# Row-wise infinity norm: the last quarter of the rows in smaller pieces, and the results stored in three parts

## The chip, the core and the metric

The kernel runs on one core of a Trainium2 chip. What counts is the device time of one execution in microseconds (us). Before the change it is 644.95 us, the median of 3 runs (644.83 to 644.98).

## What is computed

The input x is a matrix of 8192 rows and 8192 columns of float32 (268.4 MB). For each row the kernel returns the largest absolute value in it, 8192 numbers in all:

```python
x = np.random.randn(8192, 8192).astype(np.float32)
return np.linalg.norm(x, ord=np.inf, axis=1)
```

Each element is read once and used in one comparison, so this is a stream through the on-chip memory: 128 partitions, each of which holds some rows.

## The kernel before

The rows are cut into A = 8 blocks of 1024 rows. In a block each partition owns 8 consecutive rows. A block is loaded in N = 4 steps; a step loads B = 2 rows per partition, that is, 128 partitions by 64 KB, 8.39 MB, into one tile `t`. There are 32 such tiles in all, one after the other in the loops on lines 45 and 47 (the branch `if split` is never taken, since `split` is False).

Two engines take part, and the DMA engines between them:

- SP (SyncE) issues the load of each tile on line 70, all on its own DMA queue, and waits in program order. The pool `sbuf` (line 39) has three buffers. So the load of tile i+3 waits until the reduce of tile i has read the buffer.
- DVE (VectorE) reduces a tile with one instruction (lines 71 to 76) of 128 partitions by 16384 elements, which gives two maxima per partition, one for each row. They go to `r_all`, which holds all results on chip.
- When all 32 tiles are reduced, SP stores `r_all` with one DMA (line 78). It is made of runs of 8 floats (32 bytes): 8 blocks times 128 partitions, 1024 runs.

Each DMA signals its completion on a semaphore. There are eight of them, named `DMAHW0` to `DMAHW7`, which the framework hands to the DMAs in turn. A DMA that gets one of them again has to wait until the DMA that had it before is complete. In the listings below, a name in brackets is a wait, and the `_49` behind it belongs to the name alone. A wait on `DVE_49` is one for reduces that are done with.

Of the kernel before, what the change touches and what calls it, by code (L numbers as in the profile page):

```python
# [1 line left out]
logging.getLogger("concourse").setLevel(logging.ERROR)  # L3

# [1 line left out]

# [4 lines left out]


@with_exitstack
def kernel(
    ctx: ExitStack,
    tc: tile.TileContext,
    x: bass.AP,
    out: bass.AP,
    A: int = 8,
    B: int = 2,  # L20
    K: int = 4,
    BUFS: int = 3,
):
    nc = tc.nc
    P = nc.NUM_PARTITIONS

    rows, cols = x.shape
    assert rows % P == 0
    n_tiles = rows // P

    assert n_tiles % (A * B) == 0
    N = n_tiles // (A * B)
    x_t = x.rearrange("(a p n b) c -> a n p (b c)", p=P, a=A, n=N, b=B)
    out_t = out.rearrange("(a p n b) -> p a n b", p=P, a=A, n=N, b=B)

    bc = cols * B
    c_k = bc // K

    sbuf = ctx.enter_context(tc.tile_pool(name="sbuf", bufs=BUFS))
    outp = ctx.enter_context(tc.tile_pool(name="outp", bufs=1))  # L40

    r_part = outp.tile([P, N, K], mybir.dt.float32)
    r_all = outp.tile([P, A, N, B], mybir.dt.float32)

    for a in range(A):
        split = False
        for n in range(N):
            t = sbuf.tile([P, bc], x.dtype)
            t_b = t.rearrange("p (b c) -> p b c", b=B, c=cols)
            src = x_t[a, n]  # L50
            if split:
                for k in range(K):
                    nc.sync.dma_start(
                        out=t[:, k * c_k : (k + 1) * c_k],
                        in_=src[:, k * c_k : (k + 1) * c_k],
                    )
                    nc.vector.reduce_max(
                        out=r_part[:, n, k : k + 1],
                        in_=t[:, k * c_k : (k + 1) * c_k],
                        axis=mybir.AxisListType.X,  # L60
                        apply_absolute_value=True,
                    )
                nc.vector.reduce_max(
                    out=r_all[:, a, n, :],
                    in_=t_b[:],
                    axis=mybir.AxisListType.X,
                    apply_absolute_value=True,
                )
            else:
                nc.sync.dma_start(out=t[:], in_=src)  # L70
                nc.vector.reduce_max(  # L71
                    out=r_all[:, a, n, :],
                    in_=t_b[:],
                    axis=mybir.AxisListType.X,
                    apply_absolute_value=True,
                )

    nc.sync.dma_start(out=out_t[:], in_=r_all[:])


# [1 line left out]
_INS = ['x']  # L82
_OUTS = [((8192,), 'float32')]


# [23 lines left out]
```

## Time and profile before

| | |
|---|---|
| median of 3 runs | 644.95 us |
| span of the profiled execution, first to last instruction | 643.6 us |
| difference: what lies around the span | 1.35 us |
| DVE busy | 551.0 us, 32 reduces of 17.22 us |
| moved by the DMA engines | 268.47 MB, 417 GB/s over the span |
| last load landed, last reduce started | 623.38 us |
| last reduce ended, store issued | 640.6 us |

The profile is that of one execution. Its own time is its span, 643.6 us; the runs that were timed are 1.35 us longer, since they hold what lies ahead of the first instruction and behind the last. The DMA share is the mean busy share of 16 DMA engines. In short windows it goes above 1 and below it, as packets of 64 KB are counted where they are recorded; over 100 us it can be read as it stands. The chain of waits is followed back from the last instruction, at each step to what released it; where a load is in that chain, its time is from issue to landing, with what was queued ahead of it.

### The profile page before, as it was taken

The page shows a single profiled execution, that of the slowest core. Times are in us where ns is not written, and L with a number is a line of the kernel's source. Part 1 is how long each engine was busy: PE and PEld are TensorE (multiplying, and loading weights), DVE is VectorE, ACT ScalarE, POOL GpSimd, SP SyncE. Part 2 cuts the span into 40 slices and gives each one's busy share as a digit, 9 for nine tenths or more (in the row PEclk, how much of TensorE's full clock was granted, in tenths as well). Part 3 has the DMA queues.
Part 4 walks back from the last instruction along what each step waited for, and adds up shares of the span by engine and source line. Part 5 has one row for each costly group of instructions (what it writes and reads, how often), then busy time and mean ns, then how long its engine had stood idle before and what let it go on. Part 6 is the DMA issues. An engine that isn't in the chain of part 4 may idle for free.

```text
span 643.6 us, 139 instructions
## 1 busy us (share of the span) xinstructions
DVE 551.0 (86%) x32; POOL 0.2 (0%) x4
## 2 busy tenths in 40 slices
DVE  0588898888998888998888988888988888988888
POOL 0000000000000000000000000000000000000000
DMA  9999999999999999999999999999999999999960
GB/s 391 456 399 448 444 403 456 391 456 444 403 456 444 403 456 440 407 456 436 411 456 432 415 456 424 424 456 407 440 456 399 448 452 399 452 444 403 456 261 2
DMA packets 5648, 268.47 MB, mean 417 GB/s; under 512 B 1552, under 2 KB 1552, under 8 KB 1552
## 3 DMA queue, kind: packets, MB, share of 16 engines
q1 hardware_dynamic: 5648, 268.47, 96.6%
HBM read 268.44 MB, written 0.03 MB: 417 GB/s over the span
## 4 chain that ended last, share of the span: by engine, by line
DMA 70%; DVE 29%; issue 0%; SPq 0%
DMA t<-in_x_dram 70%; DVE r_all L71 29%; SPq L70 0%
## 5 line engine op out<-in xcount | busy, mean ns | idle before, releaser
L71 DVE TENSOR_REDUCE r_all<-t 128x2 f32<-128x16384 f32 x32 | 551.0, 17220 | 89.6 <-DMA t<-in_x_dram 89.6
L93 POOL MEMSET const-bfloat16-1.0<- 128x1 bf16 x1 | 0.1, 102 | 0.0
L93 POOL MEMSET const-uint8-127<- 128x1 uint8 x1 | 0.1, 102 | 0.0
L93 POOL MEMSET const-float32-0.0<- 128x1 f32 x1 | 0.1, 99 | 0.2 <-issue 0.2
L93 POOL MEMSET const-float32-1.0<- 128x1 f32 x1 | 0.1, 99 | 0.0
## 6 DMA issues: line engine op xcount, KB each, us to landing
t<-in_x_dram SPq DMA_DIRECT2D x32, 40.8
out_dram<-r_all SPq DMA_DIRECT2D x1, 32.0 KB, 2.2
```

The costliest lines, as they stand in the source:

```text
L71: nc.vector.reduce_max(out=r_all[:, a, n, :], in_=t_b[:], axis=mybir.AxisListType.X, apply_absolute_value=True,)
L93: nc = _bacc.Bacc("TRN2", target_bir_lowering=False, num_devices=1)
```

## The change

The first 48 of every 64 rows (24 of the 32 tiles) are loaded and reduced as before, into `r_bulk`. Their results are stored by one DMA that is issued from the queue of ACT (ScalarE) as soon as the 24th reduce is done.

The remaining 2048 rows are the tail: 16 rows per partition. A table `TAIL` says in which pieces each of the 16 rows is loaded: eight rows whole (8192 elements, 32 KB per partition), five rows in two pieces of 4096, two rows in four pieces of 2048, and the last row in pieces of 2048, 2048, 2048, 1024, 512 and 512 elements (2 KB per partition). Two rows still share a buffer, so the tail has 8 buffers' worth of data in 32 DMAs. Each piece has its own reduce. The partial maxima go to `part`, which is set to zero at the start; one more small reduce turns it into the results of 15 rows, `r_tail`, stored from ACT's queue. The partial maxima of the last row are written behind the row's own data in the buffer (which got 16 more elements for this), so that the last reduce reads the last piece and the five maxima as one run of 517 elements. Its result, `r_fin`, is stored by SP: 128 partitions by 4 bytes.

In the tail each partition owns 16 consecutive rows, so that neighbouring partitions read 512 KB apart in HBM; in the rest they read 256 KB apart, as before.

```diff
+TAIL = (
+    [[8192]] * 8
+    + [[4096, 4096]] * 5
+    + [[2048] * 4] * 2
+    + [[2048, 2048, 2048, 1024, 512, 512]]
+)
...
-    x_t = x.rearrange("(a p n b) c -> a n p (b c)", p=P, a=A, n=N, b=B)
-    out_t = out.rearrange("(a p n b) -> p a n b", p=P, a=A, n=N, b=B)
...
+    x_b = x[:split].rearrange("(a p n b) c -> a n p (b c)", p=P, a=A, n=G, b=B)
+    out_b = out[:split].rearrange("(a p n b) -> p a (n b)", p=P, a=A, n=G, b=B)
+    x_t = x[split:].rearrange("(p t b) c -> t p (b c)", p=P, b=B)
+    out_t = out[split:].rearrange("(p t) -> p t", p=P)
...
+    part = outp.tile([P, n_tail - 1, k_max], F32)
+    nc.vector.memset(part[:], 0.0)
+
+    def absmax(o, i):
+        nc.vector.reduce_max(out=o, in_=i, axis=X, apply_absolute_value=True)
 
     for a in range(A):
...
+        for n in range(G):
+            t = sbuf.tile([P, B * cols + 16], F32, tag="t")
+            nc.sync.dma_start(out=t[:, : B * cols], in_=x_b[a, n])
+            absmax(
+                r_bulk[:, a, n * B : (n + 1) * B],
+                t[:, : B * cols].rearrange("p (b c) -> p b c", b=B),
+            )
+    nc.scalar.dma_start(out=out_b, in_=r_bulk[:])
+
+    for i in range(0, n_tail, B):
+        t = sbuf.tile([P, B * cols + 16], F32, tag="t")
+        for j in range(B):
+            r = i + j
+            at = j * cols
+            last = r == n_tail - 1
+            for k, w in enumerate(TAIL[r]):
+                nc.sync.dma_start(
+                    out=t[:, at : at + w], in_=x_t[i // B][:, at : at + w]
+                )
+                if last and k == k_last - 1:
+
+                    absmax(r_tail[:, : n_tail - 1], part[:])
+                    nc.scalar.dma_start(
+                        out=out_t[:, : n_tail - 1], in_=r_tail[:, : n_tail - 1]
                     )
+                    absmax(r_fin[:], t[:, at : B * cols + k_last - 1])
+                elif last:
+                    absmax(
+                        t[:, B * cols + k : B * cols + k + 1], t[:, at : at + w]
                     )
+                else:
+                    absmax(part[:, r, k : k + 1], t[:, at : at + w])
+                at += w
+    nc.sync.dma_start(out=out_t[:, n_tail - 1 :], in_=r_fin[:])
```

Two places in the order of the instructions matter below. The first is on SP, the engine that issues all loads, where the tail has begun. Before, the last loads there were these, one per tile, each behind the reduce that frees its buffer, with the one store behind them:

```order
L70 DMA t<-in_x_dram 128x16384 [waits DMAHW1_49,DVE_49]
L70 DMA t<-in_x_dram 128x16384 [waits DMAHW2_49,DVE_49]
L70 DMA t<-in_x_dram 128x16384 [waits DMAHW3_49,DVE_49]
L70 DMA t<-in_x_dram 128x16384 [waits DMAHW4_49,DVE_49]
L78 DMA out_dram<-r_all 128x8x8 [waits DVE_49]
```

Now, on SP, the third, fourth and fifth tile of the tail (27th to 29th of all 32) are issued so:

```order
L82 DMA t<-in_x_dram 128x8192 [waits DMAHW7_49,DVE_49]
L82 DMA t<-in_x_dram 128x8192
L82 DMA t<-in_x_dram 128x8192 [waits DMAHW1_49,DMAHW0_49,DVE_49]
L82 DMA t<-in_x_dram 128x8192
L82 DMA t<-in_x_dram 128x4096 [waits DMAHW4_49,DMAHW3_49,DVE_49]
L82 DMA t<-in_x_dram 128x4096 [waits DMAHW2_49]
L82 DMA t<-in_x_dram 128x4096 x2
```

The fourth tile of the tail overwrites the buffer of the first, so the waits on `DMAHW0` and `DMAHW1` say that the two loads of the first tile had these; the fifth overwrites the second, whose loads had `DMAHW3` and `DMAHW4`. What came between them and took `DMAHW2` is the store of `r_bulk` on ACT's queue. So the second load of the fifth tile, the tenth of the tail, waits for that store, and all later loads stand behind it on SP.

The second place is the end of the program on DVE, where the reduces stand. Before, the last were two-row reduces of whole tiles:

```order
L71 TENSOR_REDUCE r_all<-t 128x2 [waits DMAHW4_49]
L71 TENSOR_REDUCE r_all<-t 128x2 [waits DMAHW5_49]
L71 TENSOR_REDUCE r_all<-t 128x2 [waits DMAHW6_49]
L71 TENSOR_REDUCE r_all<-t 128x2 [waits DMAHW7_49]
```

Now DVE ends with the last pieces of the row before the last one, the small reduce of `part`, and the six pieces of the last row:

```order
L63 TENSOR_REDUCE part<-t 128x1 [waits DMAHW2_49]
L63 TENSOR_REDUCE r_tail<-part 128x15 [waits DVE_49]
L63 TENSOR_REDUCE t<-t 128x1 [waits DMAHW3_49]
L63 TENSOR_REDUCE t<-t 128x1 [waits DMAHW4_49]
L63 TENSOR_REDUCE t<-t 128x1 [waits DMAHW6_49]
L63 TENSOR_REDUCE t<-t 128x1 [waits DMAHW7_49]
L63 TENSOR_REDUCE t<-t 128x1 [waits DMAHW0_49]
L63 TENSOR_REDUCE r_fin<-t 128x1 [waits DMAHW1_49,DVE_49]
```

The reduce of `part` stands ahead of all six reduces of the last row, though the source has it ahead of the last one only. Its result goes out on ACT's queue on `DMAHW5`, the name left out in the list; no load waits for that store.

More of the change, by code (lines that the diff above doesn't have):

```diff
@@ L10 @@
 from concourse._compat import with_exitstack
+F32 = mybir.dt.float32
+X = mybir.AxisListType.X
+TAIL = (
[4 more added lines that the diff above has]
+)
 @with_exitstack
@@ L18 @@
     out: bass.AP,
-    A: int = 8,
+    G: int = 4,
     B: int = 2,
-    K: int = 4,
     BUFS: int = 3,
@@ L27 @@
     rows, cols = x.shape
[L28 to L32, printed above, removed]
-    x_t = x.rearrange("(a p n b) c -> a n p (b c)", p=P, a=A, n=N, b=B)
-    out_t = out.rearrange("(a p n b) -> p a n b", p=P, a=A, n=N, b=B)
-    bc = cols * B
-    c_k = bc // K
+    n_tail = len(TAIL)
+    assert n_tail % B == 0
+    n_bulk_rows = rows // P - n_tail
+    assert n_bulk_rows % (G * B) == 0
+    A = n_bulk_rows // (G * B)
+    split = n_bulk_rows * P
@@ L39 @@
+    x_b = x[:split].rearrange("(a p n b) c -> a n p (b c)", p=P, a=A, n=G, b=B)
+    out_b = out[:split].rearrange("(a p n b) -> p a (n b)", p=P, a=A, n=G, b=B)
+    x_t = x[split:].rearrange("(p t b) c -> t p (b c)", p=P, b=B)
+    out_t = out[split:].rearrange("(p t) -> p t", p=P)
     sbuf = ctx.enter_context(tc.tile_pool(name="sbuf", bufs=BUFS))
     outp = ctx.enter_context(tc.tile_pool(name="outp", bufs=1))
-    r_part = outp.tile([P, N, K], mybir.dt.float32)
-    r_all = outp.tile([P, A, N, B], mybir.dt.float32)
@@ L45 @@
-    for a in range(A):
[L46 to L55, printed above, removed]
-                    )
[L57 to L61, printed above, removed]
-                    )
[L63 to L76, printed above, removed]
@@ L78 @@
-    nc.sync.dma_start(out=out_t[:], in_=r_all[:])
+    k_last = len(TAIL[-1])
+    r_bulk = outp.tile([P, A, G * B], F32)
+    r_tail = outp.tile([P, n_tail], F32)
+    r_fin = outp.tile([P, 1], F32)
+    k_max = max(len(r) for r in TAIL[:-1])
+    part = outp.tile([P, n_tail - 1, k_max], F32)
+    nc.vector.memset(part[:], 0.0)
+    def absmax(o, i):
+        nc.vector.reduce_max(out=o, in_=i, axis=X, apply_absolute_value=True)
+    for a in range(A):
+        for n in range(G):
[5 more added lines that the diff above has]
+            )
```

## The prediction

> **What bounds the kernel now.** I read the page first: its totals, then the chain that ended last.
>
> ```profile
> span 643.6 us, 139 instructions
> DVE 551.0 (86%) x32; POOL 0.2 (0%) x4
> DMA packets 5648, 268.47 MB, mean 417 GB/s; under 512 B 1552, under 2 KB 1552, under 8 KB 1552
> DMA 70%; DVE 29%; issue 0%; SPq 0%
> L71 DVE TENSOR_REDUCE r_all<-t 128x2 f32<-128x16384 f32 x32 | 551.0, 17220 | 89.6 <-DMA t<-in_x_dram 89.6
> ```
>
> DVE is 86% busy and 29% of the chain, which looks as if both limits counted. The chain in order of time and the timeline show that only the last reduce does.
>
> ```profile
> 582.58 40.78 DMA t<-in_x_dram
> 623.36 0.02 issue
> 623.38 17.22 DVE r_all L71
> ```
>
> That is the end of the chain (start, us, what); the next are the reduces that the text uses, and the store, from the timeline (start, us, engine, line, and the idle time before with what ended it).
>
> ```profile
> 468.58 17.22 DVE L71 TENSOR_REDUCE r_all<-t 128x2 f32<-128x16384 f32 x1 [2.12 <-DMA t<-in_x_dram]
> ...
> 545.98 17.22 DVE L71 TENSOR_REDUCE r_all<-t 128x2 f32<-128x16384 f32 x1 [2.12 <-DMA t<-in_x_dram]
> ...
> 604.03 17.22 DVE L71 TENSOR_REDUCE r_all<-t 128x2 f32<-128x16384 f32 x1 [2.12 <-DMA t<-in_x_dram]
> 623.38 17.22 DVE L71 TENSOR_REDUCE r_all<-t 128x2 f32<-128x16384 f32 x1 [2.13 <-DMA t<-in_x_dram]
> 640.62 0.40 SPq L78 DMA_DIRECT2D out_dram<-r_all  x1
> ```
>
> A tile lands every 19.35 us (623.38 − 604.03), DVE needs 17.22 of them and waits 2.1 for the next. A load takes 40.78 from issue to landing: 2.1 us of the tile in flight and two whole tiles of 19.35. So a queue of two tiles stands ahead of each load, and a buffer that came free sooner would only lengthen it. That the DMA engines are full is what the windows say:
>
> ```profile
> 500.00:600.00 100.00, 89.34 (x6) 0.00 (x0) 1.00 0.99 430
> 640.00:644.00 4.00, 0.60 (x1) 0.00 (x0) 1.00 0.12 8
> ```
>
> The share is 0.99. Up to 623.38 us this is a stream of loads that nothing but the DMA engines sets. Behind it stand 17.22 us of the last reduce and 643.6 − 640.6 = 3.0 us of store and end. The change can shorten these 20.2 us, and can slow the stream.
>
> **The stream.** The bytes are the same and the 24 first tiles are issued as before. New in the stream are packets. The page's 5648 are 32 × 128 of loads, 1024 of the store and 33 × 16 of completions. The change adds 24 load DMAs: each DMA brings 128 / 16 = 8 packets and one completion to each of the 16 engines, so 192 and 24. The store of `r_bulk` (6 × 128 packets) and that of `r_tail` (128) now run while loads run: 48 + 1 and 8 + 1 more. In all 274 packets per engine. The price of a packet that carries hardly any data comes from the store of before: in 640 to 644 us the share is 0.12, 0.48 us per engine for (1024 + 16) / 16 = 65 packets, 7.4 ns each. 274 × 7.4 ns = **2.0 us**. The lower end is nothing: the set-up of a packet can lie beside the data of the packet ahead. Below nothing is excluded, since the share leaves no room. The upper end takes the store's whole time for its 65 packets (the first row below, of the page's list of DMAs; the next two are of the line of the loads, with the time of an issue on SP and of the landing, and the last is the shortest instruction of the page):
>
> ```profile
> out_dram<-r_all SPq DMA_DIRECT2D x1, 32.0 KB, 2.2
> L70 SPq DMA_DIRECT2D t<-in_x_dram x32: 327/328/423, 0.7 to 582.6; - x32
> DMA to landing us min/median/max: 21.9/40.8/59.7
> L93 POOL MEMSET const-float32-1.0<- 128x1 f32 x1 | 0.1, 99 | 0.0
> ```
>
> 2.2 us / 65 = 34 ns, or 9.3 us. I take the share, which leaves out the waiting for an answer.
>
> SP's issue costs nothing: 0.33 us per DMA against 0.60 us of data in the smallest piece (19.35 × 512 / 16384). The waits for the eight completion names cost nothing in the later tail either: the last load waits for the one that stands seven ahead of it, and the six between hold 4 × 2048 + 1024 + 512 elements, 11.5 us of data, against 2.5 us (21.9 − 19.35) from issue to first data. The one wait that is not of this kind is a rival below. The bulk reduces keep their 17.22 and hide under the loads as before. The memset of 60 elements lies in the first 21.9 us, in which DVE has nothing to do.
>
> **The last reduces.** The 17.22 us go, but not down to one short reduce, since DVE is only 11% faster than the stream and pays a fixed part per instruction. The trace has one size of reduce, so I split it by the nearest short instruction, POOL's memset of one element, 0.10 us: (17.22 − 0.10) / 16384 = 1.045 ns per element. With the 0.02 us of "issue" in the chain between landing and start, 4096 elements take 4.40 us, 2048 take 2.26, 1024 take 1.19 and 512 take 0.66. They land 2.42 us apart for 2048 elements (19.35 / 8), with the packets above (9 × 7.4 ns, less what a whole tile's 9 had) 2.48; 1024 take 1.27 and 512 take 0.67.
>
> The last piece of 4096 is reduced 4.40 us after it landed. Eleven pieces of 2048 follow. Each shortens DVE's delay by 0.22, until it is the piece's own 2.26: after eight it is 2.64; the reduce of `part` (0.10 + 0.06 + 0.02 = 0.18) stands ahead of the ninth, so 2.60, then 2.38 and 2.26. The piece of 1024 ends 2.18 after its landing, and the two of 512, of which the last has 517, leave **2.2 us** where 17.2 stood. Without any fixed part it is 1.8; with twice it (0.20) it is 4.3, since then DVE gains nothing on the stream and carries its delay to the end. If packets cost nothing, pieces come faster and the delay is 3.4, so the two terms make up for each other: 0 + 3.4 against 2.0 + 2.2.
>
> **The end.** The last store has 9 packets per engine in place of 65, 56 × 7.4 ns = 0.41 us less, and is issued in 0.33 in place of 0.40: 3.0 − 0.5 = **2.5 us**. Two bounds: 3.0 if all of it is waiting, 2.0 if half of the 2.2 goes.
>
> **The sum.** 623.38 + 2.0 + 2.2 + 2.5 = 630.1 us of span, against 643.6. The median shown lies 1.35 us above this execution's span; with that, **631.4 us**, 2.1% less than 644.95. The low bounds (0 of packets with 1.9 of delay, 2.0 of end) give 628.6, the high ones (9.3, 4.3, 3.0) give 641.3.
>
> **Rivals.**
>
> *The store of `r_bulk` holds up the loads.* It is issued at 468.58 + 17.22 = 485.8 us, into engines that have two tiles of loads queued, and the tenth load of the tail waits for its completion, with all others behind it on SP. If an engine takes one packet from each queue in turn, each of the store's 49 packets waits for one of 32 KB, 19.35 / 16 = 1.21 us, so 59 us, to about 546. The ninth load has data until 545.98 + 4.84 = 550.8, and the tenth needs 2.5 us from issue: just in time. With two packets of loads per turn it is late. Then the loads run dry at 550.8; only then does the store get the engines, 0.5 us for its packets and 1.3 for its answer (of the old store's 2.2 with 0.4 of issue and 0.5 of packets taken off), and 2.5 until data flow: 4.3 us, **635.7 us**. It cannot be much more, since a dry queue is what frees the store. For it: the queue of 40 us, and the wait in SP's order. Against it: nothing in the trace, where two queues never ran together. The Trainium skill ("DMA: Bandwidth & Descriptors", Queues, rings and completion order) has the engines go round the queues by packets of some 9 to 17 descriptors. By that the store would need only 3 to 6 turns, under 8 us, and there would be no stall. No trace here shows it, and the sum does not rest on it.
>
> *The tail's layout slows its loads.* Neighbouring partitions read 512 KB apart instead of 256 KB. The trace shows 430 GB/s at 256 KB and nothing at 512. The tail is 8 × 19.35 = 154.8 us, so each per cent is 1.55 us. A small loss, of 3 to 4%, adds 5.4 us: **636.8 us**. The Trainium skill speaks for it ("DMA: Bandwidth & Descriptors", Latency and other measured facts): copies whose partitions are 512 KiB apart in HBM ran at 207 GB/s, where 214 was full rate. By that page my estimate is 3.4%, 5.2 us more. Those copies read and write HBM; here it is only read.
>
> *Slower than before: the same layout at a high price.* [...] The gain is 13.5 us, so it decides from 13.5 / 154.8 = 8.7% of the tail's rate, 430 down to 393 GB/s. At 15% the time is 631.4 + 23.2 = **654.6 us**; half the rate would add 155. Against it: from nothing that the trace shows is the present pitch, a power of two as well, a burden, at a share of 0.99. The difference is in the address alone, so it can neither be excluded nor sized.
>
> That the change doesn't do what it says is excluded by the order on SP and DVE: 32 loads and 33 reduces stand where 8 of each stood.
>
> **How the numbers follow.** The forecast has 0.70, the store's stall 0.10, the small loss by layout 0.13, the large one 0.05, and a loss by layout that just eats the gain 0.02. A change of under 0.2% (1.3 us) is what a measurement of this kernel can't tell from none. So faster 0.70 + 0.10 + 0.13 = 0.93, same 0.02, slower 0.05. The range goes from 629, near the low bounds, to 638, which takes in the two middle cases and half of the way to the high bounds; the large loss and the far ends are left out.
>
> **What would show it.** Right: bulk reduces that start every 19.35 us and the first tail pieces with them; a last landing at about 625.4 us; a chain whose last reduce is 0.6 to 0.7 us long, with DVE busy without a break over the last few pieces of 2048; the span's end 2.5 us behind it. A reduce of 2048 elements at 2.2 to 2.3 us would confirm the split. The store's rival shows as a hole in the DMA share near 551 us and as a wait of the tenth tail load on the store of `r_bulk`; the layout's as pieces of 8192 that land more than 9.7 us apart from the first tail tile on. A last landing after 635 us would make the prediction wrong by its stream, a DVE delay of over 4.3 us by its reduces.

## The result, and the profile after

The changed kernel takes 629.88 us (median of 4 runs, 629.82 to 630.38), the kernel before in the same runs 644.97 us (644.83 to 645.02): a ratio of 0.9768, 95% interval 0.9754 to 0.9782. It is 15.1 us faster, 2.3%. Forecast were 631.4 us, in a range from 629 to 638. A ratio leaves out a run that is over 1.5% above the fastest of its kernel, which here is one run of one experiment, of 671.77 us.

The page of the changed kernel, its totals and the chain by engine:

```profile
span 628.1 us, 196 instructions
DVE 552.7 (88%) x58; POOL 0.2 (0%) x4
DMA packets 9138, 268.49 MB, mean 427 GB/s; under 512 B 1968, under 2 KB 1968, under 8 KB 2352
DMA 64%; DVE 30%; another core or an unknown queue 4%; issue 1%; SPq 0%
out_dram<-r_bulk ACTq DMA_DIRECT2D x1, 24.0 KB, 57.9
```

DVE's work is 1.7 us more than before, and its share of the chain is no smaller: neither number says what happened. The timeline does (start, us, engine, line; the idle time before, with what ended it):

```profile
467.49 17.22 DVE L63 TENSOR_REDUCE r_bulk<-t 128x2 f32<-128x16384 f32 x1 [2.15 <-DMA t<-in_x_dram]
484.62 60.23 DVE L63 TENSOR_REDUCE part<-t 128x1 f32<-128x8192 f32 x7
484.74 0.44 ACTq L73 DMA_DIRECT2D out_dram<-r_bulk  x1
...
618.52 2.29 DVE L63 TENSOR_REDUCE t<-t 128x1 f32<-128x2048 f32 x1 [0.15 <-DMA t<-in_x_dram]
621.01 4.01 DVE L63 TENSOR_REDUCE t<-t 128x1 f32<-128x2048 f32 x3 [0.20 <-DMA t<-in_x_dram]
625.05 0.69 DVE L63 TENSOR_REDUCE r_fin<-t 128x1 f32<-128x517 f32 x1
625.77 0.35 SPq L99 DMA_DIRECT2D out_dram<-r_fin  x1
```

The tail's loads by their line on SP (issue in ns, least, median and longest, first and last start; then the time to landing), the one load that was issued after 611 us with its time to landing (from the list of DMAs of that window), and the tail's reduces by size (busy us, mean ns, idle before):

```profile
L82 SPq DMA_DIRECT2D t<-in_x_dram x32: 327/328/432, 446.1 to 611.2; - x32
DMA to landing us min/median/max: 12.2/30.4/42.9
```

```profile
t<-in_x_dram SPq DMA_DIRECT2D x1, 256.0 KB, 12.3
```

```profile
L63 DVE TENSOR_REDUCE part<-t 128x1 f32<-128x8192 f32 x8 | 68.9, 8677 | 0.4 <-DMA t<-in_x_dram 0.4
L63 DVE TENSOR_REDUCE part<-t 128x1 f32<-128x4096 f32 x10 | 43.6, 4412 | 0.9 <-DMA t<-in_x_dram 0.9
L63 DVE TENSOR_REDUCE part<-t 128x1 f32<-128x2048 f32 x8 | 17.6, 2275 | 0.0
L63 DVE TENSOR_REDUCE t<-t 128x1 f32<-128x512 f32 x1 | 0.7, 675 | 0.0
```

The last load is issued at 611.2 us and lands 12.3 us later, at 623.5 (the least of 12.2 us is another load's): practically where it landed before (623.38), though there are 24 more loads. The last reduce ends at 625.05 + 0.69 = 625.74, 2.2 us behind it, where it was 17.2. From there to the end of the span it is 2.4 us, where it was 3.0.

One wait is new. It is of SP, on the store of the first 48 rows, and the DMA share around its end shows whether it mattered:

```profile
SPq L82 <- DMA out_dram<-r_bulk: 23.2, 1, 23.2
```

```profile
540.00:545.00 5.00, 4.86 (x1) 0.00 (x0) 1.00 0.94 403
545.00:550.00 5.00, 4.76 (x1) 0.00 (x0) 1.00 0.99 423
550.00:555.00 5.00, 5.00 (x2) 0.00 (x0) 1.00 1.00 429
```

The store landed at 484.74 + 57.9 = 542.6 us, and the engines had loads all the time. So the chain of waits leads through this store (the 4% under "another core or an unknown queue"), and yet it costs nothing, as the first experiment shows.

### The profile page after: what moved, and what is told of

It reads as the page before. It is cut to its first block, busy times and chain, and to the rows that moved or that the text cites. A ratio compares the mean times of both kernels' runs of the same rounds, so it can differ in the third digit from the quotient of the medians.

```text
span 628.1 us, 196 instructions
## 1 busy us (share of the span) xinstructions
DVE 552.7 (88%) x58; POOL 0.2 (0%) x4
## 4 chain that ended last, share of the span: by engine, by line
DMA 64%; DVE 30%; another core or an unknown queue 4%; issue 1%; SPq 0%
DMA t<-in_x_dram 64%; DVE r_bulk L63 23%; DVE part L63 5%; DVE t L63 1%; SPq L82 0%; DVE r_fin L63 0%; SPq L68 0%
## 5 line engine op out<-in xcount | busy, mean ns | idle before, releaser
L63 DVE TENSOR_REDUCE r_bulk<-t 128x2 f32<-128x16384 f32 x24 | 413.3, 17219 | 70.5 <-DMA t<-in_x_dram 70.5
L63 DVE TENSOR_REDUCE part<-t 128x1 f32<-128x4096 f32 (+2 forms) x26 | 130.0, 5067 | 1.3 <-DMA t<-in_x_dram 1.3
L63 DVE TENSOR_REDUCE t<-t 128x1 f32<-128x2048 f32 (+2 forms) x5 | 8.6, 1746 | 0.4 <-DMA t<-in_x_dram 0.4
## 6 DMA issues: line engine op xcount, KB each, us to landing
out_dram<-r_bulk ACTq DMA_DIRECT2D x1, 24.0 KB, 57.9
```

What stands on the lines that cost most here:

```text
L63: nc.vector.reduce_max(out=o, in_=i, axis=X, apply_absolute_value=True)
```

## The experiments

Times are medians; the kernel before stood at 644.87 to 644.96 us beside them. Where a diff is against another experiment, it says so.

### All stores on SP's queue

```diff
-    nc.scalar.dma_start(out=out_b, in_=r_bulk[:])
...
+        if i == 2 * B:
+            nc.sync.dma_start(out=out_b, in_=r_bulk[:])
...
-                    nc.scalar.dma_start(
+                    nc.sync.dma_start(
                         out=out_t[:, : n_tail - 1], in_=r_tail[:, : n_tail - 1]
```

> The changed kernel with all three stores on SP's queue: the store of the first 48 rows per partition is issued behind the loads of the third tail tile, the store of the 15 tail rows behind the last load. Nothing else differs. In the changed kernel the store on ACT's queue took 57.9 us and the tenth load of the tail waited 23.2 us for it. Theory A (that wait is hidden, since the loads still had data until about 550 us when it ended at 542.7): the time stays within 0.5 us of 629.9, and the store takes about 42 us, the two tiles of loads that stand ahead of it, with no wait of a load for it. Theory B (the wait, or a second queue as such, costs something): 2 us or more go, to 628 or less.

629.96 us, ratio 0.9771 (0.9757 to 0.9786), a span of 628.1 us to the tenth as in the changed kernel. The store took 40.6 us, about the time of the two tiles of loads ahead of it. So the new wait and the second queue cost nothing: theory A.

### Twice as many packets in the store

```diff
-    G: int = 4,
+    G: int = 2,
```

> The changed kernel with the first 48 rows per partition in blocks of 4 rows instead of 8, so that their store on ACT's queue has runs of 16 bytes instead of 32: 96 packets per engine instead of 48, with the same bytes and the same loads. Theory A (an engine takes one packet of each queue in turn, about 1.2 us per packet of the store, and the tenth tail load waits for the store): the store would need 97 x 1.2 = 116 us, the loads run dry near 550 us, the store ends only then, 66 to 68 us after its issue, and the stream stands still for about 4 us: 633.5 to 635. Theory B (the store's 57.9 us come from the loads that were queued ahead of it, three tiles of 19.35 us): it takes 58 us again and the time stays at 629.9 to 630.4.

634.21 us, ratio 0.9836 (0.9821 to 0.985): 4.3 us slower than the changed kernel. The page, SP's waits, and the DMA share in short windows:

```profile
out_dram<-r_bulk ACTq DMA_DIRECT2D x1, 24.0 KB, 66.6
```

```profile
SPq L82 <- DMA out_dram<-r_bulk: 31.9, 1, 31.9
```

```profile
547.00:549.00 2.00, 2.00 (x1) 0.00 (x0) 1.00 0.95 402
549.00:551.00 2.00, 2.00 (x1) 0.00 (x0) 1.00 0.17 5
551.00:553.00 2.00, 2.00 (x1) 0.00 (x0) 1.00 0.49 123
553.00:555.00 2.00, 2.00 (x2) 0.00 (x0) 1.00 0.89 377
```

The store was issued at 484.46 us and landed at 551.1. From 549 on the engines stand almost still; the store ends, SP goes on, and by 553 the loads are back. The views add up the trace's records of single packets. These show it directly: until 543 us the store's packets begin 16 at a time every 1.21 us, one for each engine (twice as many when a load's completion passes), some 580 of its 1536 begin between 548.9 and 549.7, and from 549.7 to 552.0 no packet is at work. The stall, its place and its end are those of theory A: the store took one turn per packet beside the loads, was not done when the ninth load was, and got its last packets through only when the loads had run dry. Theory B had 58 us for the store. In the changed kernel 48 turns ended 7 us ahead of that point.

### The same on SP's queue, whole and in two halves

These two were to show that the 4.3 us come from the wait alone. The first is the kernel with all stores on SP, with `G` of 2:

> The kernel with 96 packets per engine in the store of the first 48 rows (blocks of 4 rows), but with all stores on SP's queue: the same loads and packets as in the run that took 634.2 us, only the store is no longer on a queue of its own that takes turns with the loads. Theory A (the 4.3 us are the wait of a load for that store): 630.0 to 630.6. Theory B (they come from the other layout of the loads or from the packets as such): 634.

633.54 us, ratio 0.9823 (0.9808 to 0.9838). Theory A was wrong: without any load that waits for the store, 3.6 us are lost again. The line of the tail's loads on SP, and DMA share and GB/s over 5 us, first of this run, then of the run with runs of 32 bytes in the same place (the first experiment):

```profile
L80 SPq DMA_DIRECT2D t<-in_x_dram x32: 327/328/20827, 446.4 to 612.3; - x32
```

```profile
525.00:530.00 5.00, 4.31 (x2) 0.00 (x0) 1.00 1.22 208
525.00:530.00 5.00, 5.00 (x2) 0.00 (x0) 1.00 1.03 434
```

The loss is elsewhere, just behind the store's packets (they begin between 525.0 and 526.1), and it is no hole: the engines are busy and move half as much. In the records of single packets the 16 load packets of 32 KB that begin next, one per engine, take 2.9 to 4.0 us, where one takes 1.21 in the run beside it. SP also spent 20.8 us inside one issue. The second run tested whether that issue was the cause:

```diff
+        if a == A - 3:
+            nc.sync.dma_start(out=out_b[:, : A // 2], in_=r_bulk[:, : A // 2])
...
-            nc.sync.dma_start(out=out_b, in_=r_bulk[:])
+            nc.sync.dma_start(out=out_b[:, A // 2 :], in_=r_bulk[:, A // 2 :])
```

> The kernel with 16-byte runs and all stores on SP, which took 633.5 us, with the store of the first 48 rows cut in two halves of 48 packets per engine each, one issued behind the 18th tile, the other where the whole store was. In the run with one store, SP was held for 20.8 us inside the issue of the load that came behind the store, and that load landed late. Theory A (SP is held since the queue takes no more packets until some are done, and 97 in one DMA are too many; so the 3.6 us are a late load): no issue takes longer than about 4 us, 630.0 to 630.6. Theory B (runs of 16 bytes, or blocks of 4 rows, cost the time as such, here and in the run of 634.2): 633 to 634 again.

633.1 us, ratio 0.9818 (0.9802 to 0.9835). The longest issue fell to 11.8 us, the time hardly, so theory A falls here too. The reduces behind the two halves:

```profile
391.07 17.22 DVE L63 TENSOR_REDUCE r_bulk<-t 128x2 f32<-128x16384 f32 x1 [2.86 <-DMA t<-in_x_dram]
410.71 17.22 DVE L63 TENSOR_REDUCE r_bulk<-t 128x2 f32<-128x16384 f32 x1 [2.42 <-DMA t<-in_x_dram]
...
538.16 8.69 DVE L63 TENSOR_REDUCE part<-t 128x1 f32<-128x8192 f32 x1 [0.68 <-DMA t<-in_x_dram]
```

Each half makes the loads right behind it late: the first costs about 1 us (2.86 + 2.42 against twice 2.13 of idle DVE), the second the rest. The packets show the same as with the whole store: behind the first half load packets of 64 KB take up to 3.3 us in place of 2.42, behind the second those of 32 KB up to 2.7 in place of 1.21. While SP was held no engine ran out of packets. The store of 32-byte runs in the same place cost nothing (the first experiment). So a block of 16-byte runs in the loads' own queue slows the loads directly behind it; why, these runs do not show. For the run of 634.2 us it leaves the wait as the cause: there the 16-byte packets went one by one, every 32 KB packet of loads that began between 500 and 548 us took 1.21 us, and what was lost is the time without any packet and the start behind it. But the control that was to prove it has a cost of its own, and so the reading rests on that run's trace alone.

### Neighbouring partitions 2 MB apart, and 512 KB apart throughout

```diff
-    x_b = x[:split].rearrange("(a p n b) c -> a n p (b c)", p=P, a=A, n=G, b=B)
...
-    x_t = x[split:].rearrange("(p t b) c -> t p (b c)", p=P, b=B)
...
+    n_b = n_bulk_rows // B
+    x_all = x.rearrange("(p t b) c -> t p (b c)", p=P, b=B)
...
+    x_b = x_all[:n_b].rearrange("(a n) p e -> a n p e", n=G)
+    x_t = x_all[n_b:]
...
```

(The lines left out do the same for the views of the result and its store.)

> The changed kernel with each partition owning 64 consecutive rows, so that neighbouring partitions read 2 MB apart in all 32 tiles, in place of 256 KB in 24 and 512 KB in 8. The store of the first 48 rows becomes 128 runs of 192 bytes, 9 packets per engine. Theory A (the loads are set by the DMA engines, whatever the distance in HBM): tiles still land every 19.35 us, 629.4 to 630. Theory B (the distance costs, by the Trainium skill's page on DMA 164 where 214 is full rate at 2 MB, an estimate of 23%): over 700 us.

677.11 us, ratio 1.0494 (1.0477 to 1.0512), 47 us slower than the changed kernel. Neither number was right: the distance does cost, but not 23% all along. The page's rate in 40 slices:

```profile
GB/s 317 359 382 379 425 410 402 421 425 417 437 425 429 437 433 429 440 433 433 433 429 410 425 425 433 437 433 429 429 404 393 411 425 389 392 364 323 269 237 108
```

It costs at the start, next to nothing in the middle, and most of all at the end, where the pieces are small. It is not that loads were issued too late, for in the slow tail too the engines were busy:

```profile
628.00:660.00 32.00, 18.18 (x9) 0.00 (x0) 1.00 0.99 255
```

The packets themselves took longer. By the records of single packets one of 64 KB took 2.95 us (median) between 10 and 30 us and 2.42 between 200 and 260; one of 8 KB, in the tail, took 0.49, where the changed kernel has 0.31. To tell place from size, the kernel before was run with the same distance, whole tiles only:

```diff
-    A: int = 8,
+    A: int = 1,
```

> The kernel before with each partition owning 64 consecutive rows: whole tiles only, neighbouring partitions 2 MB apart. With the changed kernel's tail this distance gave 677.1 us: 18 us were lost in the first eight intervals of the whole tiles, none in the next sixteen, and some 30 in the tail, most in the pieces of 4096 and less. Theory A (engines that keep in step collide, and small loads, of which eight are in flight, bring them into step again, while whole tiles let them drift apart): only the start costs, 18 to 20 us over 644.9, 663 to 666, and the last eight tiles land every 19.3 to 19.6 us. Theory B (it is the place of the last rows in HBM): the last eight tiles are as late as there, 22 to 24 us apart, 690 or more.

657.84, 658.32 and 664.51 us, and once 671.77: it scatters more than any other. The ratio is 1.0237 (1.0186 to 1.0288). The first and the last landings of the run of 658.32 us, by the reduces:

```profile
27.46 17.22 DVE L71 TENSOR_REDUCE r_all<-t 128x2 f32<-128x16384 f32 x1 [27.46 <-DMA t<-in_x_dram]
49.84 17.22 DVE L71 TENSOR_REDUCE r_all<-t 128x2 f32<-128x16384 f32 x1 [5.16 <-DMA t<-in_x_dram]
...
617.45 17.22 DVE L71 TENSOR_REDUCE r_all<-t 128x2 f32<-128x16384 f32 x1 [2.14 <-DMA t<-in_x_dram]
636.77 17.22 DVE L71 TENSOR_REDUCE r_all<-t 128x2 f32<-128x16384 f32 x1 [2.10 <-DMA t<-in_x_dram]
```

The second tile is 22.4 us behind the first, the last 19.3 behind the one ahead of it. So it is not the place of the last rows: whole tiles lose at the start, small pieces lose again at the end. In all this run lost 14.1 us (636.77 against 622.70 in the second profile of the kernel before, below), 12.5 of them up to the eighth tile, which is less than the 18 to 20 of theory A. That engines which keep in step collide, and that small pieces keep them in step, would fit this, but is not shown: the trace has no addresses.

For the distance that the change really uses, 512 KB, the first 24 tiles got it as well (`G` of 8):

> The changed kernel with 16 consecutive rows per partition in the first 24 tiles as well, so that neighbouring partitions read 512 KB apart throughout (the store of their results becomes 24 packets per engine with runs of 64 bytes). At 2 MB apart the first seven intervals between landings were 20.1 to 22.9 us, and the small pieces at the end landed up to twice as far apart as they should. Theory A (512 KB costs nothing, as the tail of the changed kernel says): tiles land every 19.3 us from the first on, 629.5 to 630. Theory B (the cost grows with the distance, and shows where the engines start together): the first intervals are 19.5 to 20.5 us, 631 to 636.

630.23 us, ratio 0.9772 (0.9757 to 0.9786), 0.35 us over the changed kernel; the tiles landed 19.3 to 19.4 us apart from the second on, the first 0.3 us later. 512 KB costs next to nothing.

### The price of the pieces

Loads of the eight whole rows cut in 16, reduces unchanged (against the first experiment):

```diff
-                nc.sync.dma_start(
-                    out=t[:, at : at + w], in_=x_t[i // B][:, at : at + w]
-                )
+                step = 512 if w == cols else w
+                for b in range(at, at + w, step):
+                    nc.sync.dma_start(
+                        out=t[:, b : b + step], in_=x_t[i // B][:, b : b + step]
+                    )
```

> The kernel with all stores on SP, where each of the eight whole rows of the tail is loaded in 16 DMAs of 512 elements instead of one; the reduces are as in the changed kernel. That is 120 DMAs more, 9 packets each per engine, with the same bytes. Theory A (about 7 ns per packet, as the prediction had it from the old store's share): 7.6 to 8.0 us more, 637.5 to 638. Theory B (34 ns per packet, the prediction's upper end): 36 us more, 666. Theory C (packets of load hide beside the data): less than 2 us more.

638.51 us, ratio 0.9901 (0.9885 to 0.9918): 8.55 us more than with whole rows, for 120 × 9 packets: 7.9 ns each. That is theory A, 0.5 us above its range. With eight completion names only eight such loads can be on their way at a time, but it is not that which slows them, since the engines were busy throughout:

```profile
540.00:550.00 10.00, 7.80 (x2) 0.00 (x0) 1.00 1.06 388
```

The same last row, but nothing ahead of it that tapers (against the first experiment):

```diff
-    [[8192]] * 8
-    + [[4096, 4096]] * 5
-    + [[2048] * 4] * 2
+    [[8192]] * 6
+    + [[4096, 4096]]
     + [[2048, 2048, 2048, 1024, 512, 512]]
...
+        if len(TAIL[i]) == 1:
+            nc.sync.dma_start(out=t[:, : B * cols], in_=x_t[i // B])
+            absmax(
+                part[:, i : i + B, 0],
+                t[:, : B * cols].rearrange("p (b c) -> p b c", b=B),
+            )
+            if i == 2 * B:
+                nc.sync.dma_start(out=out_b, in_=r_bulk[:])
+            continue
...
-        if i == 2 * B:
-            nc.sync.dma_start(out=out_b, in_=r_bulk[:])
```

> Only the last of the 32 tiles in pieces: 4096, 4096 and then 2048 three times, 1024, 512, 512, the last row as in the changed kernel. The 31 tiles ahead are whole loads and whole reduces; stores on SP as in the run with all stores there. Theory A (DVE gains on the stream only 11% and carries its delay on): the whole reduce of tile 31 ends 17.2 us after its landing, the pieces' reduces take 17.7 us more, and the last ends 15 us behind the last landing: 642 to 643.5. Theory B (the size of the last piece alone sets the end): 2 to 3 us behind the last landing, 629 to 631.

642.79 us, ratio 0.9969 (0.9955 to 0.9982). The loads of the last tile on SP (of the two smallest also the page's time to landing), and the end on DVE:

```profile
L88 SPq DMA_DIRECT2D t<-in_x_dram x8: 328/438/17952, 581.3 to 603.4; - x8
```

```profile
t<-in_x_dram SPq DMA_DIRECT2D x2, 256.0 KB, 19.1
```

```profile
602.81 25.87 DVE L62 TENSOR_REDUCE part<-t 128x2 f32<-128x16384 f32 x3 [2.23 <-DMA t<-in_x_dram]
628.60 8.38 DVE L62 TENSOR_REDUCE t<-t 128x1 f32<-128x2048 f32 x5
637.01 0.69 DVE L62 TENSOR_REDUCE r_fin<-t 128x1 f32<-128x517 f32 x1
```

From the start of the last whole tile at 602.81 DVE never rests, and the last reduce, though of 0.69 us, ends at 637.70. The last load, issued at 603.4, landed about 19.1 us later, at 622.5. The same last six pieces that end 2.2 us late behind a long taper end some 15 us late without one. Theory A, within its 642 to 643.5.

Rows whole to the end (against the first experiment):

```diff
-    [[8192]] * 8
-    + [[4096, 4096]] * 5
-    + [[2048] * 4] * 2
-    + [[2048, 2048, 2048, 1024, 512, 512]]
+    [[8192]] * 16
```

> All 16 rows of the tail loaded and reduced whole, one at a time (8192 elements), stores on SP: no smaller piece. Theory A (the delay of the last reduce behind the last landing can't be below the reduce of the last piece, and pieces of one size bring it down to that): 8.7 us behind the last landing, 16 DMAs fewer (1.0 us less of stream): 635.0 to 636.0.

636.21 us, ratio 0.9866 (0.985 to 0.9882), 0.2 us over the range that was expected:

```profile
613.11 8.69 DVE L60 TENSOR_REDUCE part<-t 128x1 f32<-128x8192 f32 x1 [0.97 <-DMA t<-in_x_dram]
622.76 8.69 DVE L60 TENSOR_REDUCE r_fin<-t 128x1 f32<-128x8192 f32 x1 [0.76 <-DMA t<-in_x_dram]
```

DVE waits 1 us for each piece: the delay has come down to the piece's own time and stays there. So loads and reduces of one row at a time bring 8.7 of the 15 us, the smaller pieces the rest.

Then a finer taper, for a version that beats the changed kernel (against the first experiment):

```diff
-    + [[4096, 4096]] * 5
-    + [[2048] * 4] * 2
-    + [[2048, 2048, 2048, 1024, 512, 512]]
+    + [[4992, 3200]] * 3
+    + [[4352, 3840]]
+    + [[3200, 2816, 2176]]
+    + [[2944, 2688, 2560]]
+    + [[2176, 1792, 1664, 1536, 1024]]
+    + [[1280, 1152, 1152, 1152, 1024, 896, 768, 768]]
```

> The kernel with all stores on SP and another table for the last eight rows of the tail: 4992+3200 three times, 4352+3840, 3200+2816+2176, 2944+2688+2560, 2176+1792+1664+1536+1024, and 1280+1152+1152+1152+1024+896+768+768: 35 loads in the tail instead of 32, each piece about as much smaller than the one ahead of it as DVE is faster than the stream. Theory A (DVE's delay at the end is the time of the last pieces, and each DMA adds 65 ns to the stream): the last reduce ends about 1.0 us behind the last landing instead of 2.1, the stream is 0.2 us longer: 0.9 us less, 629.0. Theory B (2.2 us is a floor of something else, the landing of the last pieces for instance): 630.0 as with the old table.

629.72 us, ratio 0.9765 (0.975 to 0.9779): not to be told from the changed kernel. The tail's loads on SP, and the last reduce:

```profile
L83 SPq DMA_DIRECT2D t<-in_x_dram x35: 327/328/3519, 446.4 to 614.4; - x35
DMA to landing us min/median/max: 9.9/31.2/43.0
```

```profile
624.78 0.96 DVE L66 TENSOR_REDUCE r_fin<-t 128x1 f32<-128x775 f32 x1
```

The last landing is at 614.4 + 9.9 = 624.3, the last reduce ends at 624.78 + 0.96 = 625.74, 1.4 us behind it. The delay is 0.8 us shorter, nearly as meant, and the last landing 0.8 us later than the 623.5 of the first experiment, where 0.2 had been expected. Of this, 0.3 us stood there at the 24th tile already; the other 0.3 beyond the packets is not explained. Nothing tried here beats the changed kernel by more than the measurement can tell.

### The kernel before, profiled again

> The kernel before, profiled once more. In its first profile the 24th tile was reduced from 468.58 us on, in the four kernels with the same 24 tiles that were profiled since from 467.2 to 467.5 us, though these loads are issued alike. Theory A (the first profile happened to have some slow tiles early on, 19.4 to 19.7 us apart between the 3rd and the 6th): the 24th reduce starts near 467.5 now and the last near 622.3, a span of 642.5. Theory B (the kernel before is slower there by itself, by its buffers' place for instance): 468.3 to 468.8 again and a span of 643.6.

One run, 644.96 us, a span of 642.9 us.

```profile
467.90 17.22 DVE L71 TENSOR_REDUCE r_all<-t 128x2 f32<-128x16384 f32 x1 [2.12 <-DMA t<-in_x_dram]
...
622.70 17.22 DVE L71 TENSOR_REDUCE r_all<-t 128x2 f32<-128x16384 f32 x1 [2.12 <-DMA t<-in_x_dram]
```

Between the two theories, nearer to A: 0.7 us of the first profile's 468.58 and 623.38 was that one execution's. The other 0.4 us to the changed kernel's 467.49 remain; whether its buffers, 64 bytes further apart, have to do with it was not tried. In this one execution the time around the span is 644.96 − 642.9 = 2.1 us. So the 1.35 us of the table before are not that time alone: they set the median against the profile of another execution, which was 0.7 us slower than this one.

## Why the prediction was right, point by point

The time came out 1.5 us under the forecast, near the low end of the range. The last landing was 1.9 us early and the end 0.1 shorter; the time around the span was 0.45 longer. The gain itself, 15.0 us of delay behind the last landing and 0.6 of the end, came nearly as forecast (15.0 and 0.5).

**The stream.** Forecast was a last landing at 623.38 + 2.0 = 625.4 us; it was 623.5. The price per packet held: 7.4 ns from the old store's share, 7.9 measured. The term was still too large. From the 24th landing to the last it took 623.5 − 467.5 = 156.0 us, against 154.8 for eight tiles of 19.35: 1.2 us, not 2.0, for the tail's 274 packets. The 216 of them that belong to loads make 1.6 at 7.4 ns alone, so 0.4 us even of these were not paid, and nothing that shows was paid for the 58 of the stores. With the stores in the loads' own queue the last landing was no later (608.8 + 14.7 = 623.5), so it is not the second queue that hid them; what did is not settled. And the base was too late by 1.1 us, of which 0.7 was one execution's, as the second profile shows. That 0.7 is no error on the change: the time around the span, forecast at 1.35, was 629.88 − 628.1 = 1.8 for the same reason, since the profile of before was slow against its median.

**The last reduces.** Forecast 2.2 us, measured 2.2. The exact hit has some luck in it: the split of the 17.22 us was a little off and the error cancelled. From 8677 ns for 8192 elements and 675 for 512 the slope is 8002 / 7680 = 1.042 ns and the fixed part 0.14 us, not 0.10; but of the seven reduces in a row, 60.23 us in all, each starts (60.23 − 8.68) / 6 = 8.59 us behind the one ahead, 0.09 before that one ends. So DVE gained a little more per piece than forecast, and waited 0.15 and 0.20 us for the last pieces of 2048. The bound of 4.3 us was worked out rightly, but not for the reason given: even with twice the fixed part a piece of 2048 takes 2.35 us (17.02 × 2048 / 16384 + 0.20 + 0.02) against 2.48 between landings, so DVE still gains, only too little to use up its delay. The working of the delay as a queue, by which each piece takes up what the taper ahead left over, is what the three runs with other tapers bear out: 15 us without one (expected 15), 8.7 with rows (expected 8.7), 1.4 with the finer one (expected 1.0).

**The end.** 2.5 forecast, 2.4 measured.

**The store's stall.** The forecast had the store done at about 546, just in time; it was 542.6. The mechanism was right, its point was shown by doubling the packets, and its price, 4.3 us, came out as 4.3. The rule of the Trainium skill that I set beside it ("DMA: Bandwidth & Descriptors", Queues, rings and completion order), some 9 to 17 descriptors of one queue before the engine switches, does not hold for these packets. My "under 8 us" was a wrong reading of it, as it gave the loads one descriptor per turn only: with nine of the loads' as well, a turn lasts 9.7 us, and 3 to 6 turns are, as an estimate by that page, 29 to 58 us. So the store's 57.9 us alone don't decide. What does is when its packets ran. In the records of single packets of the changed kernel's trace they begin evenly from 488 to 542 us, about 16 in every 1.21 us (twice as many when a load's completion passes): one per engine in the time of one 32 KB packet of loads, and not nine at a time every 9.7 us.

**The layout.** The small loss, 5.4 us, did not come: 512 KB apart throughout cost 0.35 us in the median. The rule on pitch of the same page (Latency and other measured facts), 207 where 214 is full, would have cost 5.2 and is not borne out for loads alone at 512 KB. The large loss is real at 2 MB, where it took 47 us, 7.5% more time; the page's 164 of 214 would be, as an estimate, 30% more time. So the slower rival named a real danger, but at four times the distance that this change uses. Why the packets take longer at that distance the traces don't show.

## What to carry to other kernels

Where a stream sets the pace and a slightly faster engine follows it, the last step can't be cut by cutting the last piece: each piece must be so much smaller than the one ahead as the engine is faster than the stream, so the taper is long (here a quarter of the work for 15 us), and each extra DMA costs its packets. A small store on a second queue was served here one packet per turn of the big loads, and took that long; look what waits for its completion name. Before rows are given to partitions in larger blocks, look how far apart the partitions then read.

## What the runs showed of the hardware that was not expected

- Loads from 128 partitions that are 2 MB apart ran at 317 to 382 GB/s at first, at about 430 after some 170 us, and down to 237 and less in the last slices with small pieces; in whole tiles the end was at full rate. The engines were busy meanwhile, with packets that took longer.
- A block of stores with runs of 16 bytes (96 or twice 48 packets per engine) in the loads' own queue delayed the loads behind it by 3 to 4 us in all, by making their next packets up to 3.3 times as long; the same bytes in runs of 32 bytes did not, nor did runs of 16 bytes on ACT's queue, one per turn.
- SP can be held inside the issue of a DMA: for 20.8 us behind a store of 96 packets per engine on its own queue, for 18.0 us behind one of 56 (in the run where only the last tile is in pieces) and for 3.5 us behind one of 48, where an issue in the changed kernel takes 0.33 to 0.44 us. How much the queue holds was not measured, and no time was lost by it in the run with 48.
- Reduces that need not wait start before the one ahead has ended: 8.59 us apart for 8.68 us of length.
